# RWKV inverse in a hybrid trunk step: updates of W and T summed in PSUM by an identity product and copied out by ScalarE, instead of subtracted by VectorE

## Chip, cores and metric

One core of one Trainium2 chip runs the whole program. The metric is the device time of one execution in microseconds (us), the median of three runs. Engines are called PE (TensorE; PEld is its weight load), DVE (VectorE), ACT (ScalarE), POOL (GpSimd) and SP (SyncE, which only issues DMAs here).

## What is computed

One inference step of a two-layer trunk on 384 tokens (128 of context, 256 latent), 1024 wide. Layer 0 mixes with an SSD head group and an RWKV-7 head group, layer 1 with a gated-linear-attention group and an mLSTM group; behind each mixer stands a squared-ReLU MLP. The change lies in the RWKV-7 group: 16 heads of 64, two scan directions, and in the reference a step-by-step recurrence:

```
def step(s, inp):
    r_t, lw_t, k_t, v_t, kk_t, a_t = inp
    s_kk = jnp.einsum('bhvk,bhk->bhv', s, kk_t)
    s = (s * jnp.exp(lw_t)[:, :, None, :] - s_kk[..., None] * (kk_t * a_t)[:, :, None, :]
         + v_t[..., None] * k_t[:, :, None, :])
    return s, jnp.einsum('bhvk,bhk->bhv', s, r_t)
```

The kernel computes it in chunks of 64 tokens (six chunks of 64 make the 384 columns). In a chunk the steps depend on one another through a unit triangular 64x64 matrix, one for each head, chunk and direction, and the kernel inverts these.

## The kernel before

The program is recorded in Python by generators, then put in order by a scheduler, engine by engine, and each engine works its list strictly in that order. `ab_streams` makes the first mixer as a pipeline of 19 slots, 16 of which hold an inverse. In a slot several streams run side by side: `fill` (dense projections: a weight panel lands by DMA as `raw`, ACT rounds it to `wH`, DVE subtracts to get `wL`, and PE makes three products of each panel into the PSUM tile `dps`; also `mod`, the adaLN products), `prep` (`rw_shared`, `rw_prep`: decays and gates, many exponentials on ACT, then the products `psc`), `inv` (`rw_tokmajor`, then `rw_inverse` of the pair prepared a slot earlier), `chain` (`rw_chain`, the scan over chunks, products `pr`, `pu`, `pd`, `py`), the SSD core (`aux`) and a tail. `run` draws the next piece from the stream that lags most behind its share; a piece ends at a `yield`. The last slots' inverse ends at about 802 us of the span; what follows (second half of the output projection, MLP, second layer, MLP) has no part in the change.

`rw_inverse(d, st)` handles two heads at once, on partitions 0 to 63 and 64 to 127, and six chunks side by side: its tiles are 128x384. It keeps two approximations in fp16, `W` (of the transposed inverse) and `T` (of the inverse), and doubles the solved block size m from 2 to 32 in five steps. In one step:

- `pz`: six 128x128 products of the masked off-diagonal part `AO` with `T`, into PSUM;
- ACT copies them in two halves into the block-diagonal tile `Zb` (`acopy`, line 277);
- after a `yield`, `pw2` (shown as `pw` in the profile): six 128x128 products of `Zb` with `W`, left out in the last step; `pt2` (shown as `pt<-Zb,W`): twelve 64x64 products of `W` with `Zb`;
- DVE subtracts: W2 = W - pw (not in the last step), then T2 = T - pt (both `tt`, line 235). The next step's `pz` needs the new T.

`W` and `T` have two buffers each, and `pz`, `pw2`, `pt2` take turns in the two PSUM banks of `self.psi`. There are 16 inverses, so 80 steps, 64 of which update W. Behind the steps a correction uses an identity in fp16, `i128h` (128x128), which adds T into the PSUM tile `pe` (line 1351). `mm` (line 221) issues one weight load and one product; `act` (line 245) is ACT's general form, `acopy` (line 277) its plain copy.

Of the kernel before, what the change touches and what calls it, by code (L numbers as in the profile page):

```python
# [13 lines left out]
AF = mybir.ActivationFunctionType  # L14
ALU = mybir.AluOpType
# [6 lines left out]
T = 384  # L22
# [153 lines left out]
class Net:  # L176
# [507 lines left out]

    def panel_raw(self, cfg, W, k0, nk, c0, ncol, placed=None):
        nc = self.nc
        raw = cfg["pool"].tile([128, nk, ncol], F32, tag="raw", name="raw", bufs=cfg["raw"])
        if placed is None:
            nc.sync.dma_start(out=raw, in_=W[128 * k0:128 * (k0 + nk), c0:c0 + ncol].rearrange("(k p) c -> p k c", p=128))
        else:  # L690
            nc.gpsimd.memset(raw, 0.0)

            src, n, step = placed
            g = ncol // step
            for k in range(nk):
                nc.sync.dma_start(out=raw[:, k].rearrange("p (g c) -> p g c", g=g)[:, :, 0:n],
                                  in_=W[128 * (k0 + k):128 * (k0 + k + 1), src:src + n * g].rearrange("p (g c) -> p g c", g=g))
        return raw
# [22 lines left out]

    def dense_cm(self, W, c0, xs, evac, placed=None, blocks=None, ncol=128, width=T, acc=None):

# [7 lines left out]
        def steps(dn):  # L731
# [18 lines left out]
            yield  # L750
        return Dense(self, [(W, k0, n, c0, ncol, placed) for k0, n in blocks], steps)

# [48 lines left out]

    def dense_tm(self, W, c0, xs, evac):

        n = self.wcfg["nk"] // 2

        def steps(dn):
            p0 = self.dacc()
            p1 = self.dacc()
            outs = [p0[:, :256], p0[:, 256:], p1[:, :256]]
            for k0 in range(0, 8, n):  # L810
                h, lo = dn.take(k0 // n)
                for i in range(3):
                    tk = slice(128 * i, 128 * i + 128)
                    for k in range(n):
                        kk = k0 + k
                        xh, xl = xs[kk]
                        self.mm(outs[i], xh[:, tk], h[:, k, :], start=kk == 0 and i != 1, stop=False)
                        self.mm(outs[i], xl[:, tk], h[:, k, :], start=False, stop=False)
                        self.mm(outs[i], xh[:, tk], lo[:, k, :], start=False, stop=kk == 7 and i != 0)
                if k0 % 2 == 0 or n > 1:  # L820
                    self.step_late()
                    yield
            evac(outs)
            yield
        return Dense(self, [(W, k0, n, c0, 256, None) for k0 in range(0, 8, n)], steps)
# [447 lines left out]
    def rw_inverse(self, d, st):  # L1273
# [8 lines left out]
        halves = (slice(0, 64), slice(64, 128))  # L1282
        A = [st["Q"][h, e, :, 0, :] for e, h in enumerate(halves)]
        i64 = self.c("i64")
        f = lambda ap: ap.rearrange("p c t -> p (c t)")
        b6 = lambda ap: ap.unsqueeze(1).to_broadcast([ap.shape[0], 6, 64])
        h6 = lambda nm, bufs: rp.tile([128, 6, 64], F16, tag=nm, name=nm, bufs=bufs)

        def heads(name, lhs, rhs):
            p = self.psi(name)  # L1290
            for c in range(6):
                for h in halves:
                    self.mm(p[h, 64 * c:64 * c + 64], lhs[h, c, :] if lhs.shape[1] == 6 else lhs[h, :],
                            rhs[h, c, :] if rhs.shape[1] == 6 else rhs[h, :])
            return p[:, :T]

        def pairs(name, lhs, rhs):
            p = self.psi(name)
            for c in range(6):
                self.mm(p[:, 64 * c:64 * c + 64], lhs[:, c, :], rhs[:, c, :])  # L1300
            return p[:, :T]

        for h, a in zip(halves, A):
# [10 lines left out]
        W = h6("W", 2)  # L1314
# [3 lines left out]
        pt = heads("pt", W, self.i64h)  # L1318
        Tm = h6("T", 2)
# [3 lines left out]
        for n, m in enumerate((2, 4, 8, 16, 32)):  # L1323
            pz = pairs("pz", self.AOb[n % 2], Tm)
            Zb = self.Zb
            zv = pz.rearrange("p (c t) -> p c t", c=6)
            for h in halves:
                self.acopy(Zb[h, :, h], zv[h])
            yield
            if m < 32:  # L1330
                pw = pairs("pw2", Zb, W)
            pt = self.psi("pt2")
            for c in range(6):
                for h in halves:
                    self.mm(pt[h, 64 * c:64 * c + 64], W[h, c, :], Zb[h, c, h])
            T2 = h6("T", 2)
            if m < 32:
                W2 = h6("W", 2)
                self.tt(f(W2), f(W), pw, ALU.subtract)
                W = W2  # L1340
            self.tt(f(T2), f(Tm), pt[:, :T], ALU.subtract)
            Tm = T2
            if n < 3:
                off(n + 2)
            if n == 0:
                for h, a in zip(halves, A):
                    self.tt(self.ALb[h, :, h], a, self.AHb[h, :, h], ALU.subtract)
            yield
# [6 lines left out]
        pt = heads("pt", Tm, self.i64h)  # L1355
        E = h6("AO", 1)
        self.tt(E, b6(i64), pe[:, :T].rearrange("p (c t) -> p c t", c=6), ALU.subtract)
        W = h6("W", 2)
# [1214 lines left out]
```

## Time and profile before

| what | value |
|---|---|
| median of 3 runs | 1857.7 us (1857.14 to 1858.3) |
| the profiled execution, its time and its span | 1855.77 us, 1853.7 us |
| PE busy over the span | 1763.3 us (95%), 13667 products |
| PE weight loads busy | 1479.4 us (80%) |
| DVE busy | 1302.7 us (70%) |
| ACT busy | 1068.7 us (58%) |
| POOL busy | 216.8 us (12%) |
| chain that ended last, whole span | PE 76%, DVE 10%, ACT 8%, issue 3% |

How to read it: the span is cut at will into stretches, and in each the busy time of an engine is the union of its instructions. Products of PE overlap, since the next one starts before the last one's end; so a product's own duration says little of its price in a row of products, and the distance from one start to the next says more. The chain of waits is followed back from the last instruction to whatever released it.

### The profile page before, as it was taken

To read this page: it belongs to the slowest core of one execution; us is meant where nothing else is said; L and a number is where in the kernel's file an instruction comes from. 1 tells how busy PE (TensorE), PEld (TensorE's weight loads), DVE (VectorE), ACT (ScalarE), POOL (GpSimd) and SP (SyncE) were. 2 spreads that over 40 slices of the span, in tenths; PEclk is the share of its full clock that TensorE was granted. 3 is DMA by queue.
4 is the path that set the end of the run, shared out by engine and by line. 5 is a ranking of instruction groups with operands and counts; after the bars stand their busy time and mean duration, and the time that the engine had idled before them with its cause. 6 is when DMAs were issued, how large, how long until landed. Compare 5 with 4: busy or idle time off the path is not lost.

```text
span 1853.7 us, 37402 instructions
## 1 busy us (share of the span) xinstructions
PE 1763.3 (95%) x13667; PEld 1479.4 (80%) x13667; DVE 1302.7 (70%) x2992; ACT 1068.7 (58%) x2688; POOL 216.8 (12%) x270
## 2 busy tenths in 40 slices
PE   7879999999999999999999999899999998999998
PEld 3677767666666777786999997889989897999887
DVE  3698788777877888768765335686786958766434
ACT  3567475747564776646654332676676756755322
POOL 3222111120112011111000000020211212000000
PEclk9889999999999999999999999999999998999999
DMA  8332443333334322345445544333333233344432
GB/s 280 114 87 75 122 136 87 106 93 112 100 103 125 99 60 86 100 129 161 126 125 176 164 143 107 84 98 103 101 94 92 74 109 106 115 125 126 149 135 80
DMA packets 314107, 213.55 MB, mean 115 GB/s; under 512 B 39648, under 2 KB 297494, under 8 KB 313924
## 3 DMA queue, kind: packets, MB, share of 16 engines
q1 hardware_dynamic: 308756, 208.35, 38.5%
q10 hardware_dynamic: 4816, 2.69, 0.5%
q8 instruction: 107, 1.75, 0.4%
q14 instruction: 76, 0.62, 0.1%
q0 software_dynamic: 352, 0.13, 0.0%
HBM read 201.32 MB, written 9.78 MB: 114 GB/s over the span
## 4 chain that ended last, share of the span: by engine, by line
PE 76%; DVE 10%; ACT 8%; issue 3%; DMA 2%; POOL 1%; SPq 1%; DVEq 0%; ACTq 0%; POOLq 0%
PE dps L221 46%; PE o L221 7%; PE ps L221 5%; PE mod L221 3%; PE aux L221 2%; DVE wL L235 2%; PE psc L221 2%; PE py L221 1%; PE pt L221 1%; PE pr L221 1%; DVE cacc L242 1%; ACT wH L277 1%; ACT Zb L277 1%; PE pw L221 1%; PE ms L221 1%
## 5 line engine op out<-in xcount | busy, mean ns | idle before, releaser
L277 ACT ACTIVATE wH<-raw 128x256 fp32r<-128x256 f32 (+1 forms) x790 | 363.2, 480 | 430.1 <-PE dps L221 305.3
L235 DVE TENSOR_TENSOR wL<-raw,wH 128x256 fp32r<-128x256 f32 (+2 forms) x771 | 399.5, 537 | 246.3 <-ACT wH L277 242.8
L277 ACT ACTIVATE Zb<-pz 64x384 f16<-64x384 f32 x160 | 77.2, 482 | 36.2 <-PE pz L221 33.8
L242 DVE SCALAR_TENSOR_TENSOR cacc<-rows,params,cacc 128x384 f32<-128x384 f32 (+1 forms) x192 | 94.2, 491 | 0.7
L221 PE MATMUL dps<-sH,wH 128*128 128x384 f32 x232 | 85.3, 369 | 5.5 <-DVE m L235 4.9
L221 PE MATMUL dps<-sL,wH 128*128 128x384 f32 x232 | 80.0, 345 | 0.3 <-DVE sL L235 0.2
L221 PE MATMUL dps<-sH,wL 128*128 128x384 f32 x232 | 79.4, 343 | 0.5 <-DVE wL L235 0.5
L221 PE MATMUL dps<-h0H,wH 128*128 128x384 f32 (+1 forms) x147 | 59.5, 406 | 11.9 <-ACT h0H L277 7.3
L235 DVE TENSOR_TENSOR AO<-AHb,rwmask 128x768 f16<-128x768 f16 (+1 forms) x112 | 60.0, 537 | 7.4 <-PE pz L221 5.7
L235 POOL TENSOR_TENSOR BK<-BK,kkk 128x768 f32<-128x768 f32 x16 | 33.8, 2110 | 222.3 <-DVE BK L239 151.3
L221 PE MATMUL mod<-xT,cond 128*32 128x384 f32 (+1 forms) x320 | 56.2, 490 | 3.7 <-DVE Q L235 2.5
L221 PE MATMUL dps<-h6H,wH 128*128 128x384 f32 (+2 forms) x147 | 54.8, 373 | 2.7 <-ACT wH L277 2.7
L221 PE MATMUL dps<-h4H,wH 128*128 128x384 f32 (+1 forms) x147 | 54.4, 375 | 2.1 <-ACT h4H L245 2.1
L221 PE MATMUL dps<-h2H,wH 128*128 128x384 f32 (+1 forms) x147 | 54.8, 374 | 0.0
L235 POOL TENSOR_TENSOR gDb<-gb 128x384 f32<-128x384 f32 x28 | 33.2, 1187 | 172.4 <-DVE gb L2224 73.2
L221 PE MATMUL dps<-h6H,wL 128*128 128x384 f32 (+2 forms) x147 | 50.8, 346 | 1.4 <-DVE wL L235 1.4
L221 PE MATMUL dps<-h0H,wL 128*128 128x384 f32 (+1 forms) x147 | 51.9, 353 | 0.0
L221 PE MATMUL dps<-h1H,wH 128*128 128x384 f32 (+1 forms) x147 | 51.8, 352 | 0.0
L221 PEld LDWEIGHTS dps<-sH,wH 128*128 128x128 f32 x232 | 43.6, 189 | 10.1 <-issue 5.6
L221 PE MATMUL dps<-h0L,wH 128*128 128x384 f32 (+1 forms) x147 | 51.5, 356 | 0.0
L221 PE MATMUL dps<-h1H,wL 128*128 128x384 f32 (+1 forms) x147 | 51.0, 347 | 0.0
L221 PE MATMUL dps<-h1L,wH 128*128 128x384 f32 (+1 forms) x147 | 51.0, 353 | 0.0
(1163 smaller groups left out, 5455.1 us busy)
## 6 DMA issues: line engine op xcount, KB each, us to landing
raw<-in_w_mlp_up SPq DMA_DIRECT2D x64, 512.0 KB
raw<-in_w_mlp_down SPq DMA_DIRECT2D x64, 512.0 KB
raw<-in_w_in_ab SPq DMA_DIRECT2D x204, 128.0 KB
xT<-in_w_mod SPq DMA_DIRECT2D x128, 192.0 KB
raw<-in_w_in_cd SPq DMA_DIRECT2D x192, 128.0 KB
raw<-in_w_mod SPq DMA_DIRECT2D x64, 192.0 KB
raw<-in_w_mod SPq DMA_DIRECT2D x32, 256.0 KB
raw<-in_w_out_cd SPq DMA_DIRECT2D x64, 128.0 KB
```

The source lines that it names most:

```text
L221: self.nc.tensor.matmul(out, lhsT, rhs, start=start, stop=stop)
L235: (eng or self.nc.vector).tensor_tensor(out=out, in0=a, in1=b, op=op)
L242: self.nc.vector.scalar_tensor_tensor(out=out, in0=a, scalar=s, in1=b, op0=op0, op1=op1)
L277: self.nc.scalar.activation(out=out, in_=in_, func=AF.Copy)
```

## The change

In each step of the inverse the old W and the old T are now added by PE: a product with the identity `i128h`, 384 columns wide, opens the PSUM sum, and the products with `Zb` go on top. To make a sum of the difference, `Zb` is written with the scale -1.0 (`act`, line 245). The sums are rounded to fp16 by an ACT copy, which is the new W or T, in place of DVE's subtractions. The order of the two is turned round as well: the sum of T and its copy come first, then those of W.

```diff
-        def pairs(name, lhs, rhs):
+        def pairs(name, lhs, rhs, plus=None):
             p = self.psi(name)
+            if plus is not None:
+                self.mm(p[:, :T], self.i128h, f(plus), stop=False)
             for c in range(6):
-                self.mm(p[:, 64 * c:64 * c + 64], lhs[:, c, :], rhs[:, c, :])
+                self.mm(p[:, 64 * c:64 * c + 64], lhs[:, c, :], rhs[:, c, :], start=plus is None, stop=plus is None or c == 5)
             return p[:, :T]
...
             for h in halves:
-                self.acopy(Zb[h, :, h], zv[h])
-            yield
+                self.act(Zb[h, :, h], zv[h], AF.Copy, scale=-1.0)
+            yield
+            pt = self.psi("pt2")
+            self.mm(pt[:, :T], self.i128h, f(Tm), stop=False)
+            for c in range(6):
+                for e, h in enumerate(halves):
+                    self.mm(pt[h, 64 * c:64 * c + 64], W[h, c, :], Zb[h, c, h], start=False, stop=c == 5)
+            Tm = h6("T", 2)
+            self.acopy(f(Tm), pt[:, :T])
             if m < 32:
-                pw = pairs("pw2", Zb, W)
-            pt = self.psi("pt2")
-            for c in range(6):
-                for h in halves:
-                    self.mm(pt[h, 64 * c:64 * c + 64], W[h, c, :], Zb[h, c, h])
-            T2 = h6("T", 2)
-            if m < 32:
-                W2 = h6("W", 2)
-                self.tt(f(W2), f(W), pw, ALU.subtract)
-                W = W2
-            self.tt(f(T2), f(Tm), pt[:, :T], ALU.subtract)
-            Tm = T2
+                pw = pairs("pw2", Zb, W, W)
+                W = h6("W", 2)
+                self.acopy(f(W), pw)
```

Pieces and yields stay as many as they were, but the scheduler orders the engines' lists anew. Three places in one slot (the one whose inverse stands at about 520 us in the trace) show it. First PE, where the second step's products stand between the gate products `pa` and the state transposes `pst`. Before:

```order
L221 MATMUL pa<-adt,lora 128x384 x2
L221 MATMUL dps<-h0H,wH 128x384
...
L221 MATMUL pu<-R,WF 64x64
L221 LDWEIGHTS Zb
L221 MATMUL pw_8019<-W,Zb 128x64
...
L221 LDWEIGHTS W
L221 MATMUL pt_8026<-Zb,W 64x64
...
L221 MATMUL pu<-R,WF 64x64 x3
```

And now:

```order
L221 MATMUL pa<-adt,lora 128x384 x2
L221 LDWEIGHTS i128h
L221 MATMUL pt_8100<-T,i128h 128x384
L221 MATMUL dps<-h0H,wH 128x384
L221 LDWEIGHTS W
L221 MATMUL pt_8100<-Zb,W 64x64
L221 MATMUL dps<-h0L,wH 128x384
...
L221 LDWEIGHTS i128h
L221 MATMUL pw_8116<-W,i128h 128x384
L221 LDWEIGHTS Zb
L221 MATMUL pw_8116<-W,Zb 128x64
```

T's identity product moved ahead of the dense products, one of the twelve `pt<-Zb,W` products stands alone between two `dps` products, the other eleven follow five `dps` later, and W's identity stands right ahead of the `pw` products. Over the whole list, T's identity stands directly ahead of its own `pt<-Zb,W` products in 46 of 80 steps and ahead of other work in 34; W's stands ahead of its `pw` products in all 64. In those 34 steps the twelve `pt<-Zb,W` products are in two parts or more, one product alone in the first; before, this was so for 11 of the `pt` groups, and for 5 of the `pw` groups, 16 in all.

Second DVE, at the same place (`UV` belongs to the chain, `S_` to `pst`). Before:

```order
L235 TENSOR_TENSOR W<-W,pw_8019 128x384
L235 TENSOR_TENSOR W<-W,sg 128x384
L235 TENSOR_TENSOR T<-T,pt_8026 128x384
L239 TENSOR_SCALAR UV<-pu 64x2x64
L1159 COPY S_8090<-pst 128x128
```

And now:

```order
L235 TENSOR_TENSOR lw<-b,lw 128x384
L235 TENSOR_TENSOR W<-W,sg 128x384
L239 TENSOR_SCALAR UV<-pu 64x2x64
L1159 COPY S_8173<-pst 128x128
L239 TENSOR_SCALAR BK<-ta,bks 128x6x64 x2
```

The two subtractions are gone from DVE's list (`W<-W,sg` is another tile of that name, of the SSD part). Third ACT, at the same place (`ta` and `xT` are the gates of `rw_shared`). Before:

```order
L245 ACTIVATE ta<-ta 128x384
L245 ACTIVATE xT_8008<-xT_8008 128x384
L245 ACTIVATE UV<-pu 64x2x64
L277 ACTIVATE Zb<-pz 64x6x64 x2
L277 ACTIVATE wH<-raw 128x256 x3
```

And now:

```order
L245 ACTIVATE ta<-ta 128x384
L245 ACTIVATE xT_8089<-xT_8089 128x384
L277 ACTIVATE T<-pt_8100 128x384
L277 ACTIVATE W<-pw_8116 128x384
L245 ACTIVATE UV<-pu 64x2x64
L245 ACTIVATE Zb<-pz 64x6x64 x2
L277 ACTIVATE wH<-raw 128x256 x2
```

The copies of T and W stand behind the six gate activations and ahead of the next two halves of `Zb`.

## Rows read from the trace of the kernel before

**Rows 1.** Busy time by stretch: us, busy of each engine (instructions), clock, DMA share, GB/s

```profile
core 0: us, PE busy (x) PEld busy (x) DVE busy (x) ACT busy (x) POOL busy (x), PEclk, DMA share, GB/s
124.00:803.00 679.00, 655.36 (x7358) 478.29 (x7358) 552.63 (x1369) 427.55 (x1088) 101.23 (x108) 0.99 0.35 100
```

**Rows 2.** Chain that ended last, 124 to 803 us, by engine and line

```profile
by line: PE dps L221 28.5%; PE mod L221 6.5%; PE aux L221 5.9%; PE psc L221 4.1%; PE pt L221 3.5%; PE py L221 3.4%; PE pr L221 3.0%; ACT Zb L277 2.5%; issue 2.5%; PE pw L221 2.2%; ACT xT L245 1.9%; PE pu L221 1.7%; DVE cacc L242 1.7%; PE pz
```

**Rows 3.** Tile T: ns min/median/max, first and last start us, forms

```profile
L235 DVE TENSOR_TENSOR T<-T,pt x80: 535/546/555, 138.1 to 798.5; 128x384 f16<-128x384 f16 x80
L277 ACT ACTIVATE T<-pt x16: 471/490/510, 129.6 to 777.2; 128x384 f16<-128x384 f32 x16
L221 PE MATMUL pe<-T,i128h x16: 322/336/338, 157.4 to 799.8; 128*128 128x384 f16 x16
```

**Rows 4.** Tile W, same columns

```profile
L235 DVE TENSOR_TENSOR W<-W,pw x64: 526/548/557, 137.6 to 794.6; 128x384 f16<-128x384 f16 x64
...
L277 ACT ACTIVATE W<-pt x16: 467/484/499, 158.7 to 800.8; 128x384 f16<-128x384 f32 x16
```

**Rows 5.** Timeline of PE, one inverse step: start us, us, what, tile of the array, shape

```profile
537.63 0.35 PE L221 MATMUL pw<-W,Zb 128*128 128x64 f16 x6 [0.31 <-ACT Zb L277]
537.91 0.38 PE L221 MATMUL pt<-Zb,W 64*64 64x64 f16 x12
538.21 0.34 PE L221 MATMUL pd<-UV,BKT 128*64 128x64 f32 x4
```

**Rows 6.** Timeline of PE, changes from one kind of product to another

```profile
525.93 0.35 PE L221 MATMUL pz<-T,AO 128*128 128x64 f16 x6
526.11 0.42 PE L221 MATMUL dps<-h4L,wH 128*128 128x384 f32 x1
526.37 0.33 PE L221 MATMUL dps<-h4H,wL 128*128 128x384 f32 x1
526.54 0.34 PE L221 MATMUL dps<-h5H,wH 128*128 128x384 f32 x1
...
541.16 0.34 PE L221 MATMUL dps<-h5H,wL 128*128 128x384 f32 x1
541.43 0.33 PE L221 MATMUL pr<-S,KR 64*64 64x64 f32 x4
...
543.70 0.33 PE L221 MATMUL pe<-T,i128h 128*128 128x384 f16 x1
543.86 0.19 PE L221 MATMUL pe<-T,AHb 128*128 128x64 f16 x1
```

**Rows 7.** Timeline of PE, one pt product alone between dense products

```profile
460.49 0.33 PE L221 MATMUL dps<-h1L,wH 128*128 128x384 f32 x1
460.75 0.21 PE L221 MATMUL pt<-Zb,W 64*64 64x64 f16 x1
460.90 0.44 PE L221 MATMUL dps<-h1H,wL 128*128 128x384 f32 x1
461.18 0.33 PE L221 MATMUL dps<-h2H,wH 128*128 128x384 f32 x1
```

**Rows 8.** Waits of PE, 124 to 803 us: us in total, times, longest

```profile
PE pw L221 <- ACT Zb L277: 3.1, 5, 1.3
PE psc L221 <- DVE BK L235: 2.9, 2, 2.7
PE pz L221 <- DVE T L235: 2.7, 4, 0.9
PE mod L221 <- DVE Q L235: 2.5, 3, 1.5
```

**Rows 9.** Timeline of ACT, first and last of six gate activations without a pause

```profile
523.81 0.58 ACT L245 ACTIVATE ta<-pa,ha 128x384 f32<-128x384 f32 x1
...
525.99 0.52 ACT L245 ACTIVATE xT<-xT 128x384 f32<-128x384 f32 x1
```

**Rows 10.** Timeline of DVE, the subtraction of T at that place

```profile
524.62 0.55 DVE L235 TENSOR_TENSOR T<-T,pt 128x384 f16<-128x384 f16 x1
```

## The prediction

> **What bounds the kernel now.** I first cut the span into stretches, because the inverse runs only from 124 to 803 us. There PE is busy for 655.36 of 679 us, DVE for 552.63 (81%), ACT for 427.55 (63%) [rows 1]. A busy PE need not be a full PE, so the second view is the timeline, from start to start. In a row of dense products one starts 0.17 to 0.18 us after the other (526.37 to 526.54) though each lasts 0.33: they overlap, and the next is issued as soon as the array can take it [rows 6]. PE's list is dense nearly everywhere. Third, the chain of waits of this stretch: its first seven entries are all PE's, `dps` alone 28.5%; the largest of ACT is `Zb` with 2.5%, and DVE's subtractions of W and T do not come among the thirteen entries printed ahead of the cut, the smallest of which has 1.7%, so each lies at or under some 12 us [rows 2]. Fourth, who makes PE wait: for DVE's T 2.7 us in four waits, for ACT's `Zb` (at `pw`) 3.1 us in five [rows 8]. So **PE bounds this stretch**, with 679 - 655.36 = 23.6 us of visible idle time. The change takes work from DVE, which rarely holds PE up, and gives some to PE.
>
> **The change part by part.**
>
> *DVE loses* 80 x 0.546 + 64 x 0.548 = 43.7 + 35.1 = 78.8 us [rows 3, 4]. Its busy share of the stretch goes from 81% to (552.63 - 78.8) / 679 = 70%. On the path lies only what PE waits for: the 2.7 us for T go, at most. Waits for other results of DVE, `BK` 2.9 and `Q` 2.5 us, may shorten as its queue gets thinner; I take half, 2.7 us (bounds 0 and 5.4) [rows 8].
>
> *ACT gains* 80 x 0.490 + 64 x 0.484 = 39.2 + 31.0 = 70.2 us, with the copies of T and W that already exist as prices [rows 3, 4]; its busy share goes from 63% to (427.55 + 70.2) / 679 = 73%. The negative scale on `Zb` I cost at nothing, since it is the same pass over the same elements. A T copy ends sooner after its products than a T subtraction that stands behind W's, but now waits in ACT's queue, and behind a T copy stand the next `Zb`, and so the next `pw` and `pt` products. The 160 `Zb` copies make PE wait 3.1 us today; with 144 more ACT results in the same loop I take 144/160 of that again, +2.8 us. The bounds are 0 and the case of the third rival below.
>
> *PE gains 144 identity products* and their weight loads. The weight loads I cost at nothing: they go beside the product ahead, as `pe`'s do. The product has a twin in the trace: `pe<-T,i128h`, same tile, same shape, x16 [rows 3]; the next product starts 0.16 us after it (543.70 to 543.86) [rows 6]. Its neighbours matter too, because a change of the array's tile costs: a dense product is followed by another after 0.17 to 0.18 us, but by the 64-row `pr` after 0.27 (541.16 to 541.43), +0.09 [rows 6].
> - A full step today: `pw` starts at 537.63, `pt` at 537.91, the next work at 538.21, so 0.28 + 0.30 = 0.58 us [rows 5]. After the change: identity of T 0.16 + 0.09 to get to the 64x64 tiles, `pt` 0.30, identity of W 0.16, and `pw`, which is now followed by a 128-row product as `pz` is at 525.93, 0.18 [rows 6]: 0.89 us. The difference, 0.31 us, comes 64 times: 19.8 us.
> - The last step (no W), 16 times: the identity's 0.16, as the way into `pt` is paid today as well: 2.6 us.
> - In 34 of the 80 steps the new order puts T's identity ahead of other work. After an fp16 product the next dense one holds PE for 0.26 (526.11 to 526.37) instead of 0.17 [rows 6]: 34 x 0.09 = 3.1 us.
> - In the same 34 steps one `pt` product stands alone, against 16 such cuts today. One of those is in the trace: from the dense product at 460.49 to that at 461.18 it takes 0.69 us with one `pt` between, where two dense distances are 0.35: +0.34 us [rows 7]. (34 - 16) x 0.34 = 6.1 us.
>
> Together **+31.6 us on PE**. No row has an identity followed by a 64x64 product, so bounds: 144 x 0.16 = 23.0 us if no change of tile shows, 144 x 0.27 + 6.1 = 45.0 us if each one pays the dearest distance above. I keep 31.6, as its parts are the nearest rows.
>
> *What idle time takes up.* Where PE waits for something that does not depend on it, more PE work ahead of the wait shortens it. The bounds are 0 and all of the 23.6 us; most of that idle time belongs to chains that go through PE itself, so I take 3 us.
>
> Here a rule speaks for the change. By the Trainium skill, "Trainium Kernel Development and Optimization", Performance Expectations, the time that matmuls are busy is a bad measure of how near a kernel is to its limit, because matmuls are pipelined; the busy share of weight loads is a better one. The weight loads are busy for 478.29 of 679 us here, 70% [rows 1], so by that rule PE would have room for the identity products, and the sum would lose its largest term (first rival). The starts 0.17 us apart [rows 6] speak against it: they are what PE can do on 384 columns, not overlap that hides free time.
>
> **The sum.** 31.6 (PE) - 2.7 (wait for T) - 2.7 (other waits for DVE) + 2.8 (waits for ACT) - 3 (idle time taken up) = +26 us. The profiled execution took 1855.77 us (a span of 1853.7 and 2.1 around it), so the changed one would take 1881.8; the median of the runs, 1857.7, is 1.9 above it, which gives 1883.7, rounded to **1884 us**. With the bounds of PE's term (23.0 to 45.0) and of the others the forecast's own range is 1866 to 1898.
>
> **The rivals.**
> 1. *PE has room, and DVE's queue was the cost.* Mechanism: the identity products fall into gaps between the starts, T comes earlier, and DVE's other results with it. For it: DVE is busy 81%, and the four waits for DVE and ACT above add up to 11.2 us [rows 8]. Against it: the dense starts, and the chain with hardly a subtraction in it. The price if the identities are free: the three waits for DVE, 2.9 + 2.7 + 2.5 = 8.1 us, and as much again for delays too short to show: 1857.7 - 16, or about 1842; with half of that, 1850. It decides if the starts of dense products around the identities do not move apart. Chance 0.10. The room by weight loads is this rival's rule.
> 2. *The two cancel.* The 23.6 us of idle time take up nearly all of the identity products: 31.6 - 23.6 - 2.7 - 2.7 = +2.6, or 1860; chance 0.08.
> 3. *ACT becomes the bound of the inverse's loop.* Place: where `rw_shared`'s gates fill ACT. Six activations run from 523.81 to 526.51 without a pause [rows 9], and in the new order the T copy stands behind them; DVE's subtraction of the same T ended at 525.17 [rows 10]. The copy would end at 526.51 + 0.49 = 527.00, 1.8 us later. Where PE has less work than that before the next `pz`, it waits. If each of 16 slots pays it once: +29 on top, or 1884 + 29 = 1913; half of it 1898. It decides when the PE work between `pt` and the next `pz` is under some 3 us. Against it: at this place the new list puts more dense products there. Chance 0.15.
>
> That the change does not do what it says is not among them: the subtractions are gone from DVE's list, and the identities stand in PE's.
>
> **How the numbers follow.** Forecast 0.67, rivals 0.10, 0.08, 0.15. About 0.2%, 3.7 us, is what a measurement of this kernel can tell from no change. Rival 1 is faster; rival 2 is the same in most of its cases, up to 1861.4; forecast and third rival are slower: 0.10, 0.08, 0.82. The range runs from rival 2's time, 1860, into the third rival, 1905: left out are the first rival and part of the second below, and the dearer third of the third above, some 0.2.
>
> **What would show it.** In the stretch of the inverses PE should have 144 more 128x384 fp16 products (`pt<-T,i128h`, `pw<-W,i128h`), with the next start about 0.16 us after one, or 0.25 where a 64x64 product follows; the stretch should get longer by about the 26 us, and the rest of the span stay as it is. DVE's busy time should fall by 79 us, ACT's rise by 70. PE's waits for T should now name ACT, with a few us in total. If PE's visible idle time falls by 15 us or more, the second rival was right; if it grows by 10 or more and names ACT's T or `Zb`, the third. The forecast is wrong if the stretch does not get longer though the 144 products are there: then PE was full only to the eye.

## The result and the profile after

The changed kernel takes **1887.16 us** (median of four runs, 1878.26 to 1889.72) against 1858.0 us for the kernel before beside it: a ratio of 1.0149, interval 1.0134 to 1.0165, or 27.7 us more. The forecast was 1884, slower. The direction and the size came out; of the terms behind them one came out in part and the others did not, as the experiments show.

The page of the kernel after, busy time of each engine over the span of 1886.5 us (of before: the table of the profile before):

```profile
PE 1802.1 (96%) x13811; PEld 1504.0 (80%) x13811; DVE 1249.0 (66%) x2848; ACT 1130.1 (60%) x2832; POOL 214.3 (11%) x270
```

The 144 products are there (13667 before) and the 144 results have moved from DVE to ACT. DVE lost 53.7 us and ACT gained 61.4, less than the 79 and 70 of the forecast; why, stands at the end. Next the windows of the kernel after, which answer to [rows 1]: us, PE, PEld, DVE, ACT, POOL busy (instructions), clock, DMA share, GB/s. The stretch of the inverses now ends at 840 us.

```profile
124.00:840.00 716.00, 694.88 (x7505) 501.50 (x7505) 499.80 (x1227) 489.33 (x1235) 98.53 (x108) 0.97 0.33 95
840.00:1886.00 1046.00, 1009.39 (x5759) 932.80 (x5757) 676.90 (x1431) 578.29 (x1433) 81.23 (x107) 0.99 0.41 118
```

The stretch takes 716 us instead of 679, +37, and what follows it 1886.5 - 840 = 1046.5 us instead of 1853.7 - 803 = 1050.7, about -4 (this profiled execution is one of the longer ones, 1888.31 us). The loss lies in the stretch, as promised, though not with +26 there and 0 behind. PE's visible idle time in it went from 23.6 to 21.1 us, so PE is as full as before, and the granted clock from 0.99 to 0.97. That last number was not in the forecast.

The chain of waits in that stretch, kernel after (answers to [rows 2]):

```profile
by line: PE dps L221 30.2%; PE pt L221 6.7%; PE mod L221 6.1%; PE aux L221 6.0%; PE psc L221 4.6%; PE pw L221 4.3%; PE py L221 4.1%; PE pr L221 3.4%; PE pu L221 2.4%; PE pz L221 2.2%; PE pd L221 1.8%; PE pbk L1260 1.7%; DVE cacc L242 1.6%; 
```

The chain is still PE's from end to end. `pt` has nearly doubled its share (3.5 to 6.7%) and so has `pw` (2.2 to 4.3%): the identities carry these names. `Zb` of ACT, 2.5% before, is no longer among the entries printed.

Tiles T and W of the kernel after (answers to [rows 3, 4]): ns min/median/max, first and last start, forms.

```profile
L277 ACT ACTIVATE T<-pt x96: 471/490/539, 130.4 to 834.1; 128x384 f16<-128x384 f32 x96
L221 PE MATMUL pt<-T,i128h x80: 323/337/503, 135.1 to 833.4; 128*128 128x384 f16 x80
```

```profile
L221 PE MATMUL pw<-W,i128h x64: 336/337/502, 135.6 to 829.3; 128*128 128x384 f16 x64
L277 ACT ACTIVATE W<-pw x64: 474/490/522, 138.7 to 830.2; 128x384 f16<-128x384 f32 x64
```

One step of the inverse on PE after the change (timeline; start us, us, product, tile of the array, shape), which answers to [rows 5]:

```profile
607.36 0.33 PE L221 MATMUL pu<-R,WF 64*64 64x64 f32 x4
607.62 0.34 PE L221 MATMUL pt<-T,i128h 128*128 128x384 f16 x1
607.89 0.38 PE L221 MATMUL pt<-Zb,W 64*64 64x64 f16 x12
608.19 0.34 PE L221 MATMUL pw<-W,i128h 128*128 128x384 f16 x1
608.37 0.34 PE L221 MATMUL pw<-W,Zb 128*128 128x64 f16 x6
608.54 0.38 PE L221 MATMUL aux<-negb,identb 128*128 128x512 bf16 x1
```

From 607.62 to 608.54 it is 0.92 us; the forecast had 0.89 for this step, and its prices are confirmed where the products stand: 0.27 from T's identity to the 64x64 products (0.25 forecast), 0.30 for these, 0.18 from W's identity to its own products (0.16), 0.17 for those. What this list costs in time is another matter.

Waits of PE in the stretch, kernel after: us in total, times, longest (answers to [rows 8]).

```profile
PE mod L221 <- DVE Q L235: 4.3, 2, 2.1
PE pt L221 <- ACT Zb L245: 2.5, 4, 1.0
PE aux L221 <- DVE ti L235: 2.4, 3, 1.1
PE psc L221 <- DVE BK L235: 2.4, 1, 2.4
PE pr L221 <- DVE S L235: 1.9, 2, 1.6
```

The waits for T (2.7 us before) are gone and none names ACT's T. Those for `Q` are longer, not shorter.

### The profile page after: what moved, and what is told of

The parts are those of the page before. It is cut to its first block, busy times and chain, and to the rows that moved or that the text cites. A ratio compares the mean times of both kernels' runs of the same rounds, so it can differ in the third digit from the quotient of the medians.

```text
span 1886.5 us, 37671 instructions
## 1 busy us (share of the span) xinstructions
PE 1802.1 (96%) x13811; PEld 1504.0 (80%) x13811; DVE 1249.0 (66%) x2848; ACT 1130.1 (60%) x2832; POOL 214.3 (11%) x270
## 4 chain that ended last, share of the span: by engine, by line
PE 82%; DVE 8%; ACT 6%; issue 2%; POOL 1%; DMA 1%; DVEq 0%; ACTq 0%; SPq 0%; POOLq 0%
PE dps L221 48%; PE o L221 7%; PE ps L221 5%; PE mod L221 3%; PE pt L221 3%; PE aux L221 2%; PE psc L221 2%; PE pw L221 2%; PE py L221 2%; DVE wL L235 2%; PE pr L221 1%; DVE cacc L242 1%; PE pu L221 1%; ACT wH L277 1%; PE pz L221 1%
## 5 line engine op out<-in xcount | busy, mean ns | idle before, releaser
L235 DVE TENSOR_TENSOR AO<-AHb,rwmask 128x768 f16<-128x768 f16 (+1 forms) x112 | 66.4, 593 | 17.8 <-PE pz L221 14.9
L221 PE MATMUL dps<-h0H,wH 128*128 128x384 f32 (+1 forms) x147 | 60.6, 413 | 11.1 <-ACT h0H L277 7.3
L277 ACT ACTIVATE T<-pt 128x384 f16<-128x384 f32 x96 | 47.1, 490 | 28.2 <-PE pt L221 26.9
L221 PEld LDWEIGHTS <-W 64*64 64x64 f16 x1152 | 30.3, 109 | 31.4 <-issue 27.8
```

Of the source, the lines that this page charges most:

```text
L221: self.nc.tensor.matmul(out, lhsT, rhs, start=start, stop=stop)
L235: (eng or self.nc.vector).tensor_tensor(out=out, in0=a, in1=b, op=op)
L277: self.nc.scalar.activation(out=out, in_=in_, func=AF.Copy)
```

## The experiments

Three things change together: identity products on PE (I), copies on ACT instead of subtractions on DVE (A), and the turned order, T ahead of W (O). Each run below was timed beside the kernel before (medians of 1858.2 to 1859.4 us), and "+" is the measured ratio put on that; its 95% interval reaches 2 to 4 us to either side. Theory A says that PE's price is the loss, B that the copies on ACT hold the loop up, C that the turned order does it.

**The changed kernel again**, with no edit.

> The changed kernel itself, beside the others on one chip. Theory A (the identity products' price on PE), theory B (the copies of T and W hold the inverse's loop up on ACT) and theory C (the turned order and the new lists cost by themselves, without identities) all expect 1880 to 1890 us, some 27 above the kernel before; its four runs lay between 1878 and 1890, and a lower mean clock went with the longer ones.

1887.88 us, ratio 1.016 (1.0141 to 1.0179), +29.7 us. The loss is there again at its size.

**Identities alone** (to the kernel before): the products behind them begin the sum anew.

```diff
+            if dead is not None:
+                self.mm(p[:, :T], self.i128h, f(dead))
...
-                pw = pairs("pw2", Zb, W)
+                pw = pairs("pw2", Zb, W, W)
             pt = self.psi("pt2")
+            self.mm(pt[:, :T], self.i128h, f(Tm))
```

> The kernel before, with the 144 identity products of T and W put in front of the pt and pw products and overwritten by them; DVE subtracts as before, ACT and its list as before, W first as before. Theory A: 19.8 + 2.6 us for the products in place and 41 x 0.09 = 3.7 for those that stand ahead of other work, +26, so 1884 us, or 1880 where idle time takes some up. Theory B: 1858 to 1861, as nothing is put on ACT. Theory C: 1858 to 1862, as the order is the old one.

1866.06 us, ratio 1.0043 (1.0028 to 1.0059), +8.0 us. That fits none of the three theories: far under A's 1880 to 1884, clear of the 1858 to 1862 of B and C. The identity products alone cost under a third of the loss. The windows of this kernel:

```profile
124.00:817.00 693.00, 670.98 (x7506) 486.35 (x7508) 555.51 (x1369) 430.44 (x1091) 101.03 (x108) 0.99 0.35 99
```

The stretch is 14 us longer, with the clock and the idle time (693 - 670.98 = 22.0 us) nearly as before. Yet the distances from each of the 144 identities to the next product on PE add up to 31.7 us in this trace. The same sum goes down by 6.5 us for `pw<-W,Zb`, and that is no slack: `pw` stood ahead of the 64x64 products (0.28 us from 537.63 to 537.91 [rows 5]) and now stands ahead of T's identity, so a change of tile that `pw` paid for has moved to the identity. Net of it 25.2 us are left, against the 26 that were expected of this run. Then the sum goes down by 5.5 us for `dps`, 3.3 for `mod`, 2.5 for `aux` and 2.2 for `pu`; in these stand shorter waits and fewer products at a low clock as well. So about half of the net price is paid by other products' starts and waits, which the view of busy time does not show.

**Without the identities** (to the changed kernel).

```diff
-            self.mm(pt[:, :T], self.i128h, f(Tm), stop=False)
...
-                    self.mm(pt[h, 64 * c:64 * c + 64], W[h, c, :], Zb[h, c, h], start=False, stop=c == 5)
+                    self.mm(pt[h, 64 * c:64 * c + 64], W[h, c, :], Zb[h, c, h])
...
-                pw = pairs("pw2", Zb, W, W)
+                pw = pairs("pw2", Zb, W)
```

> The changed kernel without the identity products: the sums leave out the old W and T, so ACT copies only the products with Zb; order and copies are those of the change, and a pt product stands alone in 36 of 80 steps. Theory A: +6 for the products that stand alone, -5 for the waits on DVE that go, so 1855 to 1862 us. Theory B: 1875 or more, as ACT's part is all there. Theory C: 1875 or more.

1866.43 us, ratio 1.005 (1.0035 to 1.0066), +9.3 us, between the theories again (A had 1855 to 1862, B and C 1875 or more): with copies and order alone a third of the loss is left, and taking the identities out of the full change gives back 18 to 20 us, more than twice what they cost alone. The parts do not simply add. (The sums leave out the old W and T here, so this is no version to use.)

**Copies on DVE** (to the changed kernel).

```diff
-            self.acopy(f(Tm), pt[:, :T])
+            nc.vector.tensor_copy(f(Tm), pt[:, :T])
...
-                self.acopy(f(W), pw)
+                nc.vector.tensor_copy(f(W), pw)
```

> The changed kernel with the copies of T and W on DVE instead of ACT (144 copies of 128x384). Theory A: as the change or a few us more, 1882 to 1890, since PE's work is the same. Theory B: back to 1858 to 1865, since ACT is as free as it was. Theory C: as the change, 1882 to 1890; it does not tell A from C, which the runs with dead and without identities do.

1867.93 us, ratio 1.0059 (1.0043 to 1.0076), +11.0 us, just above the 1858 to 1865 of theory B and far from the 1882 to 1890 of A and C. With the same products on PE, the engine that copies makes 17 to 19 us of difference, and ACT is the dear one. The lists of all engines are ordered anew with it, so this does not yet say by which way ACT costs that.

**The old order** (to the changed kernel: sum of W first, then T; W's copy first).

```diff
+            if m < 32:
+                pw = pairs("pw2", Zb, W, W)
             pt = self.psi("pt2")
...
             Tm = h6("T", 2)
             self.acopy(f(Tm), pt[:, :T])
-            if m < 32:
-                pw = pairs("pw2", Zb, W, W)
-                W = h6("W", 2)
-                self.acopy(f(W), pw)
```

(W's copy now stands ahead of the line with `Tm`.)

> The changed kernel with the old order within a step: W's sum and copy first, then T's. Identities stay; steps in which a pt product stands alone fall from 34 to 10. Theory A: the 6.1 us that I put on the lone products go, part of it comes back as T is copied behind W: 1878 to 1884 us, 3 to 8 under the change. Theory C (the turned order is the cost): 1860 to 1868.

1874.43 us, ratio 1.0082 (1.0068 to 1.0095), +15.2 us, between theory C (1860 to 1868) and A (1878 to 1884): the turned order is worth 12.5 to 14.5 us in the full change, by either measurement of that, three times what it costs alone (next run).

**The turned order alone** (to the kernel before).

```diff
-            if m < 32:
-                pw = pairs("pw2", Zb, W)
             pt = self.psi("pt2")
...
+            self.tt(f(T2), f(Tm), pt[:, :T], ALU.subtract)
+            Tm = T2
             if m < 32:
+                pw = pairs("pw2", Zb, W)
                 W2 = h6("W", 2)
                 self.tt(f(W2), f(W), pw, ALU.subtract)
                 W = W2
-            self.tt(f(T2), f(Tm), pt[:, :T], ALU.subtract)
-            Tm = T2
```

> The kernel before with only the order turned: T's products and subtraction first, then W's, all on DVE, no identities. Lone pt products in 36 steps against 16 cuts before. Theory A: (36 - 16) x 0.34 = +6.8 for the lone products, less 2.7 for T's wait: 1858 to 1866 us. Theory C: 1875 or more. If T's earlier end is worth more than the lone products, under 1856.

1861.34 us, ratio 1.0022 (1.0009 to 1.0036), +4.1 us, as theory A had it (1858 to 1866). In this kernel 36 `pt` groups are in two parts or more, and 34 of them have one product alone in front; the forecast's way of costing them gives (36 - 16) x 0.34 = 6.8 us, less up to 2.7 for T's wait.

**T by identity and ACT, W still subtracted by DVE** (to the changed kernel).

```diff
-                pw = pairs("pw2", Zb, W, W)
-                W = h6("W", 2)
-                self.acopy(f(W), pw)
+                pw = pairs("pw2", Zb, W)
+                W2 = h6("W", 2)
+                self.tt(f(W2), f(W), pw, ALU.add)
+                W = W2
```

> Only T is summed with the identity and copied by ACT; W2 = W + pw (Zb is negative) stays on DVE. 80 of the 144 identities. Theory A: 80 x 0.16 plus the 0.09 of change into the 64x64 tiles where nothing else paid it, some 15 to 19, and 6 for lone products, less 3 to 5 of waits: 1872 to 1878 us. Theory B: T's copy on ACT is the loop, so all of the change, 1885.

1871.84 us, ratio 1.006 (1.0042 to 1.0079), +11.2 us, at the lower edge of theory A's 1872 to 1878; theory B's 1885 falls. Rather more than half of the change, less than half of the loss.

**T's identity behind its products** (to the changed kernel).

```diff
-            self.mm(pt[:, :T], self.i128h, f(Tm), stop=False)
             for c in range(6):
                 for e, h in enumerate(halves):
-                    self.mm(pt[h, 64 * c:64 * c + 64], W[h, c, :], Zb[h, c, h], start=False, stop=c == 5)
+                    self.mm(pt[h, 64 * c:64 * c + 64], W[h, c, :], Zb[h, c, h], start=c == 0, stop=False)
+            self.mm(pt[:, :T], self.i128h, f(Tm), start=False)
```

> The changed kernel with T's identity behind its twelve products, so that the scheduler cannot put it ahead of other work; W's identity follows it, both 128-row products on one weight set. Lone pt products stay in 32 steps. Theory A: the 3.1 us for identities ahead of other work go, 1881 to 1884 us, 2 to 5 under the change.

1879.29 us, ratio 1.0114 (1.0098 to 1.0129), +21.2 us, 2 us under what was expected. The place of T's identity makes 6.5 to 8.5 us; the forecast had 3.1 for identities ahead of other work. The edit also puts the two identities next to each other and orders the lists anew, so not all of it need be that.

**Copies on ACT alone** (to the old-order kernel above).

```diff
-                pw = pairs("pw2", Zb, W, W)
+                pw = pairs("pw2", Zb, W)
...
-            self.mm(pt[:, :T], self.i128h, f(Tm), stop=False)
...
-                    self.mm(pt[h, 64 * c:64 * c + 64], W[h, c, :], Zb[h, c, h], start=False, stop=c == 5)
+                    self.mm(pt[h, 64 * c:64 * c + 64], W[h, c, :], Zb[h, c, h])
```

> In the old order (products and sum of W ahead of those of T), without identity products, W and T copied out of PSUM by ACT instead of subtracted by DVE; the sums leave out the old W and T. It is the last corner of the set: identities alone +8 us over the kernel before, order alone +4, order and copies +9, identities and copies +15, all three +28. Theory 1 (the copies on ACT cost by themselves, and costs add): 9 - 4 = +5 to 15 - 8 = +7 us, 1863 to 1865. Theory 2 (the copies cost nothing unless a later T copy meets the new order or a fuller PE list): within 2 us of 1858. Theory 3 (DVE's thinner queue is worth something by itself, the first rival of the prediction): under 1855.

1853.65 us, ratio 0.9973 (0.9963 to 0.9983), **-5.0 us**. So moving the 144 results from DVE to ACT is a gain by itself: theory 3 of this run holds, theories 1 and 2 fall. Its windows show DVE's share of the load down as in the full change, the same idle time as before (678 - 653.67 = 24.3 us) and a clock of 0.98:

```profile
124.00:802.00 678.00, 653.67 (x7362) 479.99 (x7360) 494.75 (x1226) 484.40 (x1233) 99.35 (x108) 0.98 0.36 101
```

This kernel leaves out part of the sum, so it is no version to use.

**T copied by DVE, W by ACT**, and **W copied by DVE, T by ACT** (to the changed kernel).

```diff
-            self.acopy(f(Tm), pt[:, :T])
+            nc.vector.tensor_copy(f(Tm), pt[:, :T])
```

> The changed kernel, with the sum of T copied out by DVE and that of W still by ACT. Both sums on DVE gave 1868, both on ACT 1884 to 1888. Theory 1 (T's copy is what holds the loop up, since the next pz needs the new T and the copy stands behind gates and Zb in ACT's queue): 1866 to 1872. Theory 2 (it is the number of results that ACT gives the loop, or its busy time): in the middle, 1875 to 1880. Theory 3 (W's copy holds it up): 1882 or more.

```diff
-                self.acopy(f(W), pw)
+                nc.vector.tensor_copy(f(W), pw)
```

> The changed kernel, with the sum of W copied out by DVE and that of T still by ACT: the mirror of the run with T on DVE. Theory 1 (T's copy on ACT is the cost): 1882 or more. Theory 2 (the number of results on ACT): 1875 to 1880. Theory 3 (W's copy on ACT): 1866 to 1872. If this one and its mirror both stay at 1868 to 1872, the cost of ACT comes only where both copies stand in its queue.

T on DVE: 1874.77 us, ratio 1.0078 (1.0056 to 1.01), +14.5 us. W on DVE: 1866.05 us, ratio 1.0051 (1.0031 to 1.0071), +9.5 us. Both copies on DVE cost 11.0, both on ACT 27.7. Theory 1 of these runs (T's copy on ACT is the cost) falls, since T's copy may stay on ACT at no cost as long as W's is off it. Theory 3 (W's copy) has the second run but misses the first by 7 us; theory 2 misses the second, and the first lies at its edge. The dear case is both copies on ACT.

**Identities and turned order, DVE subtracting** (to the kernel before in the turned order).

```diff
+            if dead is not None:
+                self.mm(p[:, :T], self.i128h, f(dead))
...
             pt = self.psi("pt2")
+            self.mm(pt[:, :T], self.i128h, f(Tm))
...
-                pw = pairs("pw2", Zb, W)
+                pw = pairs("pw2", Zb, W, W)
```

> The kernel before with DVE's subtractions, in the turned order (T ahead of W), and with the 144 identity products, which the products behind them overwrite: identities and order without the copies on ACT. Identities alone gave +8 us, order alone +4, both with DVE copies in place of the subtractions +11. Theory 1 (the two add, and the change's other +16 needs the copies on ACT): 1868 to 1872. Theory 2 (identities and order make each other dearer, as by lone products and identities ahead of other work, and the copies on ACT add nothing): 1880 or more. Theory 3 (one hides the other): under 1866.

1867.9 us, ratio 1.0047 (1.0031 to 1.0064), +8.7 us, a little under the 1868 to 1872 of theory 1, which takes this run: all of PE's new work in the new order, without ACT, is still under a third of the loss. Its windows, and then its waits of PE:

```profile
124.00:815.00 691.00, 675.68 (x7498) 487.70 (x7497) 549.42 (x1367) 429.68 (x1086) 101.72 (x108) 0.99 0.35 99
```

```profile
PE mod L221 <- DVE Q L235: 2.6, 2, 1.8
...
PE pt L221 <- ACT Zb L277: 0.8, 2, 0.5
```

PE's idle time is 691 - 675.68 = 15.3 us here, 8.3 us less than before (the identities alone, in the old order, took off 1.6), and the copies on ACT open 5.8 us again (21.1). `Q` of DVE (2.6 to 4.3), `Zb` of ACT (0.8 to 2.5) and `S` of DVE at `pr` (none to 1.9) are where.

With that the eight corners are complete. Us over the kernel before by the measured ratio, and the mean granted clock over the span in the timed runs:

| identities | order | subtracted by DVE | copied by ACT | price of the copies |
|---|---|---|---|---|
| no | old | 0, clock 0.979 | -5.0, 0.979 | -5.0 |
| no | turned | +4.1, 0.979 | +9.3, 0.976 | +5.2 |
| yes | old | +8.0, 0.981 | +15.2, 0.976 | +7.2 |
| yes | turned | +8.7, 0.981 | +27.7, 0.976 | +19.0 |

Down the last column, where each number is good to some 4 us: alone the copies gain 5 us, the turned order makes them some 10 us dearer, the identities some 12, both together 24. That is most of what the change costs: its parts by themselves add up to 7 us (8.0 + 4.1 - 5.0), the rest comes of the copies meeting the two others.

**What of this is the clock.** In every kernel the runs differ in the same way: the lower the granted clock, the longer. Through the 59 runs of the kernel before (clock 0.974 to 0.983) a straight line falls by 1.35 us for each 0.001 of clock, with a correlation of -0.93. The changed kernel fits: 1878.26 us at 0.981, 1886.02 at 0.975, 1888.31 at 0.973, 1889.72 at 0.975. From identities and order (0.9812 on average) to the full change (0.976) the clock falls by 0.005, 7 us of the 19 by that line. With all runs brought to 0.979 by it, the column on the right reads -4, +1, +3 and +11 to +12: the same pattern, a good third lower at its top.

The profiled executions show what the time of the stretch is made of. Three parts add up to it: PE's visible idle time; what the lower clock costs, which is half of the time that the clock stood at the lower of its two levels, since starts lie twice as far apart there (last section); and the rest, which is PE's products at full clock.

| kernel, with the clock of its profiled execution | stretch, us | PE idle | at the lower clock | of that lost | rest |
|---|---|---|---|---|---|
| before, 0.980 | 679 | 23.6 | 19.0 | 9.5 | 645.9 |
| identities, 0.980 | 693 | 22.0 | 19.4 | 9.7 | 661.3 |
| order, 0.978 | 687 | 24.3 | 23.1 | 11.5 | 651.2 |
| copies, 0.979 | 678 | 24.3 | 20.5 | 10.2 | 643.5 |
| identities, order, 0.983 | 691 | 15.3 | 11.1 | 5.6 | 670.1 |
| the change, 0.973 | 716 | 21.1 | 47.0 | 23.5 | 671.4 |
| the change again, 0.976 | 714 | 22.1 | 37.5 | 18.8 | 673.1 |

The last column is PE's price: the identities put 15 us there, identities and order 24, the change 25 to 27. The copies add next to nothing to it (670.1 to 671.4). Their price is waits and clock: from identities and order to the change the stretch grows by 25 us, 5.8 of them idle time and 17.9 the lower clock. This pair of executions lies 0.010 apart in clock and the averages 0.005, so such an 18 is more than usual. The end of each stretch is set by eye, to a microsecond or two.

**What PE did before the clock fell.** In the stretch of the kernel after the clock falls to the lower level seven times. Ahead of six of these, within 2 us, PE had waited: for `BK` (2.36 us, with 3.4 us at the lower level behind it, both there without the copies on ACT too), for `S` (1.59, then 3.4), for `modsb` of ACT (0.74, then 3.4; without the copies on ACT a wait of 0.77 was followed by none), for `Q` (2.15, then 10.2), for `Q` again (2.15, then 6.8) and for `Zb` (0.96, then 10.2, with a second wait of 0.74 across its start). The seventh, 6.8 us from 488.40 on, has no wait over 0.2 us in the 8 us ahead of it, and the repeat has the other six, in part of other lengths, but not this one. Without the copies on ACT (identities and order) there are two, behind `BK` and behind the first `Q` (1.81, then 6.8).

The two waits for `Q` are for DVE, whose queue the change made thinner. The second of them, in the kernel after (DVE and PE, start us, us, what, and in brackets the idle time before it and its releaser):

```profile
609.13 0.48 DVE L239 TENSOR_SCALAR cacc<-rows,params 128x384 f32<-128x384 f32 x1 [0.35 <-ACT rows L277]
609.64 3.06 DVE L242 SCALAR_TENSOR_TENSOR cacc<-rows,params,cacc 128x384 f32<-128x384 f32 x4
612.63 1.01 DVE L235 TENSOR_TENSOR Q<-psc,rwmask 128x384 f32<-128x384 f32 x2
613.23 0.85 PE L221 MATMUL mod<-xT,cond 128*32 128x384 f32 x8 [2.15 <-DVE Q L235]
```

And the same place with identities and order, DVE subtracting:

```profile
594.18 0.54 DVE L235 TENSOR_TENSOR T<-T,pt 128x384 f16<-128x384 f16 x1
594.65 0.48 DVE L239 TENSOR_SCALAR cacc<-rows,params 128x384 f32<-128x384 f32 x1
595.05 0.55 DVE L235 TENSOR_TENSOR W<-W,pw 128x384 f16<-128x384 f16 x1
595.51 1.27 DVE L242 SCALAR_TENSOR_TENSOR cacc<-rows,params,cacc 128x384 f32<-128x384 f32 x2
596.70 1.01 DVE L235 TENSOR_TENSOR Q<-psc,rwmask 128x384 f32<-128x384 f32 x2
597.30 0.85 PE L221 MATMUL mod<-xT,cond 128*32 128x384 f32 x8 [0.76 <-DVE Q L235]
```

The subtractions are gone, but the scheduler's new list has four `cacc` of that line ahead of `Q` instead of two. Counted from the `pu` products ahead (607.36 and 592.88), `Q` starts 5.27 us after them instead of 3.82. So here the copies cost through DVE's list, and not through ACT.

**How ACT's queue does it** can be seen at one of the six places; the timeline of PE and ACT, start us, us, what, and in brackets the idle time before it and its releaser:

```profile
734.12 0.49 ACT L277 ACTIVATE T<-pt 128x384 f16<-128x384 f32 x1 [0.56 <-PE pt L221]
...
734.56 0.49 ACT L277 ACTIVATE W<-pw 128x384 f16<-128x384 f32 x1
...
734.66 0.33 PE L221 MATMUL pz<-T,AO 128*128 128x64 f16 x6
...
735.67 0.53 ACT L245 ACTIVATE lw<-lw 128x384 f32<-128x384 f32 x1
...
736.09 0.53 ACT L245 ACTIVATE eI<-b 128x384 f32<-128x384 f32 x1
...
736.50 0.48 ACT L245 ACTIVATE Zb<-pz 64x384 f16<-64x384 f32 x1
736.87 0.52 ACT L245 ACTIVATE b<-b 128x384 f32<-128x384 f32 x1
...
737.03 0.19 PE L221 MATMUL pt<-Zb,W 64*64 64x64 f16 x1 [0.96 <-ACT Zb L245]
...
737.42 0.48 ACT L245 ACTIVATE Zb<-pz 64x384 f16<-64x384 f32 x1
...
737.95 0.48 PE L221 MATMUL pt<-Zb,W 64*64 64x64 f16 x11 [0.74 <-ACT Zb L245]
738.37 0.50 PE L221 MATMUL pw<-W,i128h 128*128 128x384 f16 x1
738.66 0.53 PE L221 MATMUL pw<-W,Zb 128*128 128x64 f16 x6
```

T's and W's copies go back to back through ACT, gates of another stream stand behind them, and `pz`, whose products were done at 734.99, gets its first `Zb` at 736.50 and its second at 737.42. PE waits twice, 0.96 and 0.74 us, right ahead of `pt`. The windows around that place (columns as above, the clock is the third number from the end):

```profile
730.50:733.92 3.42, 3.42 (x38) 2.28 (x35) 2.24 (x6) 2.58 (x8) 0.00 (x0) 1.00 0.27 77
733.92:737.33 3.41, 2.33 (x35) 1.84 (x30) 1.78 (x6) 3.21 (x8) 0.83 (x1) 1.00 0.42 130
737.33:747.57 10.24, 9.62 (x92) 7.10 (x91) 6.77 (x19) 6.94 (x19) 0.00 (x0) 0.51 0.13 42
```

ACT is busy for 3.21 of 3.41 us, PE for 2.33; then PE's clock is at 0.51 for 10 us, which is the lower of its two levels. At that level W's identity is followed by its own product after 0.29 us (738.37 to 738.66), against 0.18 at 608.19. So a wait of 1.7 us is followed by 10 us at half speed. That the copies made this one wait is argued from the queue. That the kernels with both copies on ACT and either of the other parts run at 0.976 on average, and those with none of them or one there at 0.979 to 0.982, is measured, with one exception: with T's sum and copy changed alone it is 0.976 too.

Of the 19 us between the medians, then, 6 to 7 are idle time and 7 to 10 the clock (7 by the line; 10 if all the time by which the average clock falls short is lost, (1 - 0.976) x 1887 - (1 - 0.9812) x 1868). Left open: the 2 to 6 us between that and 19, and why it takes both copies on ACT. No run keeps the lists as they are and moves only the copies, so how much of the 19 is ACT's queue and how much the new lists of DVE and PE is not separated.

## Why the prediction was right, and where it was not

It was right in its verdict and near in its 26 us. Part of that is its mechanism, PE's own work; the rest is luck, since two errors cancel: the identities in the new order cost 20 us less than forecast, and the copies on ACT 22 us more.

- **PE bounds the stretch**: right; the chain of after is PE's again.
- **PE's term, 31.6 us**: the prices at issue are right where the products stand, and PE's products at full clock do take 25 to 27 us more in the changed kernel; the term is some 5 us too large.
- **Idle time taken up, "I take 3 us"**: too small by itself. The run with identities and turned order holds all of PE's term and cost 8.7 us instead of 31.6 - 3 = 28.6. In its stretch PE's products take 24 us more, idle time falls by 8.3 and the loss to the lower clock by 3.9, which makes the 12 us by which it is longer. The bounds named there, 0 to 23.6 us, held the value; the choice near the lower end was wrong. By the Trainium skill, "Trainium Kernel Development and Optimization", Performance Expectations, the busy time of matmuls is a bad measure of how near a kernel is to its limit; the trace agrees in part, as 144 more products cost 8 us by themselves in a kernel whose PE was busy for 95% of the span, but it does not make them free, as the first rival had it.
- **The turned order**: 6.1 us for lone products, 4.1 measured by itself. Right. Identities ahead of other work: 3.1 us forecast, up to 6.5 to 8.5 measured by putting T's identity last, in a kernel with the copies on ACT. Too small there.
- **DVE and ACT, -2.7 - 2.7 + 2.8 = -2.6 us**: the term that failed most. For the copies alone it is close (-5.0). On top of identities and order it is +19.0. The waits for T went, as forecast. That waits for other results of DVE would shorten as its queue gets thinner is the step that failed: those for `Q` grew (2.5 us before, 2.6 without the copies, 4.3 with them), since the scheduler put other work into DVE's list where the subtractions had been. ACT's price was scaled from the old waits for `Zb`; they are 2.5 us now, but the longest place is followed by 10 us at the lower clock, and the clock is in no term of the sum.
- **The range**: the forecast's own 1866 to 1898 does not follow from the bounds given, which taken together reach further to both sides.
- **The third rival** had a mechanism that shows at one place, `Zb` and copies in one ACT queue: no wait names T, and the place shown is one where copies, then other gates, go ahead of `Zb`. Its sign, visible idle time up by 10 us or more, did not come: it fell by 2.5 us, and even against identities and order it rose by 5.8 only.
- **Busy times**, -79 and +70 forecast, -53.7 and +61.4 measured: durations were added where instructions overlap; on DVE other instructions also got longer (`AO<-AHb,rwmask` by 6.3 us in all). On ACT `lw`, `eI`, `Zb` and `b` start at 735.67, 736.09, 736.50 and 736.87, 0.37 to 0.42 apart, with durations of 0.48 to 0.53. 61.4 / 144 = 0.43 us is the price of one such copy. It had no part in the sum.
- **A count**: in the trace W's identity stands right ahead of its own products in 60 of 64 steps, not in all, and ahead of other work in four. At 0.09 us each it moves nothing.

A version that beats both kernels did not come out of this. The copies' -5 us can't be had without something that adds the old W and T, and by identity products that costs 8.

## What to carry to other kernels

Cost extra work on a full engine at its issue price, then ask by a run with the work done and thrown away how much of it is paid: here 25 us of issue, net, cost 8. A change that moves work between engines should be taken apart into all its corners, since copies that gain 5 us alone lost 19 on top of the two other edits. An engine from which work is taken away need not answer sooner when a scheduler fills its list anew: look at what stands ahead of the results that others wait for. And where PE waits inside a dense stretch, look at the granted clock behind it before costing the wait at its own length.

## What the runs showed of the hardware

The clock falls inside a stretch in which PE is 97% busy. A case of it in the kernel after, with one wait of 2.15 us for `Q` (613.23), in windows:

```profile
611.04:614.45 3.41, 1.26 (x14) 0.60 (x13) 3.37 (x7) 0.13 (x1) 1.45 (x1) 1.00 0.00 0
614.45:621.28 6.83, 6.83 (x47) 3.62 (x46) 3.75 (x13) 2.68 (x7) 1.19 (x1) 0.52 0.45 146
```

And in the kernel before, where DVE held PE up in the same way:

```profile
405.60:409.00 3.40, 1.90 (x29) 1.02 (x28) 3.40 (x7) 0.97 (x2) 1.05 (x1) 1.00 0.15 39
409.00:415.80 6.80, 6.80 (x36) 3.26 (x34) 4.81 (x16) 0.83 (x2) 0.87 (x1) 0.52 0.31 93
```

In both PE is busy without a pause while it runs at the lower level, so busy time counts these microseconds as full. Inside the low pieces of the kernel after, the distances from start to start add up to 44.0 us; the same pairs of products take 21.8 at full clock (each pair by its median in all traces), so a microsecond there does half a microsecond's work. The case without a wait, in the same columns:

```profile
484.99:488.40 3.41, 3.41 (x39) 2.79 (x38) 2.42 (x5) 2.03 (x6) 0.00 (x0) 1.00 0.69 218
488.40:495.23 6.83, 6.83 (x34) 5.50 (x36) 3.66 (x11) 4.02 (x10) 1.21 (x1) 0.50 0.19 50
```

Nor does each wait bring the clock down: in the same trace waits of 1.05 us (248.24), 1.10 (399.16) and 1.14 (586.73) had no fall behind them. The Trainium skill, "TensorE: Matmul & The Clock Gate", HAM oscillation, tells of a kernel whose waits for DMA bring the clock down again and again; in this case's trace six of the seven falls follow waits for DVE or ACT, and the runs of one kernel differ in clock and time together, by 8 to 11 us between 0.981 and 0.975 to 0.973 in the kernel after.

A change of the array's tile shows its price: from an identity to a 64x64 product 0.27 us, to a 128-row product 0.18 (607.62 and 608.19). The Trainium skill, "TensorEngine Tiling (Array Packing)", Key Properties, says that a change of tiling mode drains the engine, without a figure; these rows put 0.09 us on it.
